# A background selection on VectorE: its steps priced anew, every fourth low part on GpSimd, the gates' sums two steps later

## The chip, the cores and the metric

The kernel runs on one core of one Trainium2 chip. The metric is the device time of one execution in microseconds (us). The shown time of the kernel before is the median of three runs, 1817.89 us (1817.82 to 1819.13).

## The reference, cut to what matters

Two layers work on 256 tokens of width 1024. Layer 0 mixes with latent attention, layer 1 with a sparse attention; each is followed by a product-key expert mixer, `_peer`, and it is inside `_peer` that the change lies:

```python
q = (xt @ w_q).reshape(T, PEER_HEADS, 2, PEER_QDIM // 2)
s1 = jnp.einsum('thd,hnd->thn', q[:, :, 0], sub_keys[0])
s2 = jnp.einsum('thd,hnd->thn', q[:, :, 1], sub_keys[1])
v1, i1 = lax.top_k(s1, PEER_TOPK)
v2, i2 = lax.top_k(s2, PEER_TOPK)
cand = (v1[..., :, None] + v2[..., None, :]).reshape(T, PEER_HEADS, -1)
cand_idx = (i1[..., :, None] * PEER_NKEYS + i2[..., None, :]).reshape(T, PEER_HEADS, -1)
best, pos = lax.top_k(cand, PEER_TOPK)
expert = jnp.take_along_axis(cand_idx, pos, axis=-1)
gate = jax.nn.softmax(best, axis=-1)
...
a = jnp.einsum('td,ted->te', x_blk, w_down[e_blk])
hg = jax.nn.gelu(a, approximate=False) * g_blk
y = jnp.einsum('te,ted->td', hg, w_up[e_blk])
```

There are 8 heads, 128 keys a half, 16 chosen of each, and 128 x 128 = 16384 experts.

## The kernel before, in words

**Dense experts.** The kernel does not gather. It multiplies all 16384 rows of `w_down` with the tokens (128 blocks of 128 rows, the tile `d`, two blocks to a PSUM tile, loop over `b0`), applies Gelu, multiplies by a matrix of gates that is zero where an expert isn't chosen (tile `G`, built by one-hot matmuls), and multiplies by `w_up` (tile `y`).

**Split operands.** Every weight block of 512 KB is loaded by SyncE into one of four `raw` buffers. ScalarE rounds it to the high part (`hi`, L105), VectorE takes the difference (`lo`, L109), and TensorE multiplies three pairs: 24 matmuls of 256 columns make one block of `pq` (the queries) or `d`, in the order hi, hi, lo. The class `Stream` keeps the parts in a ring of four slots: `get()` for block i queues the parts of block i+3 and the loads up to i+6. A slot is written again when the block four places earlier has been multiplied, and a `raw` buffer is loaded again when both its parts are made. `Stream.share` says that every so many low parts GpSimd makes one (L107) instead of VectorE; before the change it is set only in layer 1's attention (3).

**The selection in the background.** While TensorE does `pq` and the first half of `d`, VectorE chooses the experts between its low parts. `choose()` (from L1054) is a generator of steps. First come 32 rounds of `top16` over 128 scores (five instructions: MAX8, FIND_INDEX8, MATCH_REPLACE8, MAX8, FIND_INDEX8, L983 to L987). Then for each of the two tiles of 128 tokens: `pairs` (16 sums of candidates on VectorE, L1009, and 16 of indices on GpSimd, L1012, then 8 rounds of `top16` over 50 candidates), `weigh` (softmax: a subtraction L994, the exponential on ScalarE L995, then sum, reciprocal and product, L997 to L999), and `experts` (for each head a comparison on VectorE, L1026, a product on GpSimd, L1029, a reduction on VectorE, L1033). At the end `gates()` turns the two results with TensorE (tile `gT`, L1042) and makes `place16` and `gate16`.

**What sets the order.** `spend(PACE)` is called once for each block from the second pair of queries on: it adds an income to a purse and runs steps while the purse is positive, each `yield` taking its price off. All of VectorE's work here is chained in the order in which it is emitted (`dve` and `link`, L243 to L257), so the prices decide how many steps stand between two low parts. Once `spend` reports that the selection is over, `prepare` (L1094 to L1104) builds one-hot tiles for four tokens a group, and `place` multiplies them into `G`; at most two groups an iteration of two blocks, 64 in all.

Of the kernel before, what the change touches and what calls it, by code (L numbers as in the profile page):

```python
# [39 lines left out]
OFF = [sum(SEG[:a]) for a in range(TOPK)]  # L40
CELLS = sum(SEG)
STAGGER = 4
PACE = 5.75
FIRST = 4
WARM = 9
EARLY = 11264
# [123 lines left out]
def tile_trunk(ctx: ExitStack, tc: tile.TileContext, ins, out: bass.AP):  # L170
# [19 lines left out]
    def ps(name):  # L190
        return psp.tile([P, 512], F32, tag="ps", name=name)

    def py(i, name):
        return pyp.tile([P, 512], F32, tag=f"py{i}", name=name)
# [26 lines left out]
    ws = Stream(nc, raws, *ring)  # L221
# [34 lines left out]
    def dve(emit):  # L256
        return link("dve", emit)  # L257
# [4 lines left out]
    def mm(o, l, r, start, stop):  # L262
        return pe(lambda: nc.tensor.matmul(o, l, r, start=start, stop=stop, skip_group_check=True))  # L263
# [10 lines left out]
    def proj(o, blk, w=P, late=False):  # L274

        h, l = blk
        if late:
            for c in range(NC):
                mm(o, h[:, c * w : (c + 1) * w], xh[:, c, :], c == 0, False)
                mm(o, h[:, c * w : (c + 1) * w], xl[:, c, :], False, False)  # L280
            for c in range(NC):
                ins = mm(o, l[:, c * w : (c + 1) * w], xh[:, c, :], False, c == NC - 1)
            return ins
        for c in range(NC):
            s = slice(c * w, (c + 1) * w)
            ins = mm3(o, (h[:, s], l[:, s]), (xh[:, c, :], xl[:, c, :]), c == 0, c == NC - 1)
        return ins
# [639 lines left out]
    def peer(li):  # L927
# [25 lines left out]
        def turn():  # L953
            for t in range(2):
                p = ps(f"qwT{t}")
                for n in range(4):
                    nc.tensor.transpose(p[:, n * P : (n + 1) * P], qrow[t][:, n * P : (n + 1) * P], ident)
                nc.scalar.copy(qT[:, 0:4, t * P : (t + 1) * P], p.rearrange("p (n t) -> p n t", t=P))

        def queries(n):  # L960
            p = ps(f"pq{n}")
            pv = p.rearrange("p (j t) -> p j t", t=T)
            first = proj(pv[:, 0, :], ws.get())
            if n == FIRST:
                with tc.issue_after(first.ins):
                    turn()
            else:
                spend(PACE)
            proj(pv[:, 1, :], ws.get())
            if n > FIRST:  # L970
                spend(PACE)
            nc.scalar.copy(qT[:, n : n + 2, :], pv)

        def scores(g4):
            for t in range(2):
                p = py((2 * g4 + t) % 4, f"ps{g4}{t}")
                for j in range(4):
                    n = 4 * g4 + j
                    mm(p[:, j * P : (j + 1) * P], qT[:, n, t * P : (t + 1) * P], keys[:, n, :], True, True)
                nc.scalar.copy(s[t][:, 4 * g4 : 4 * g4 + 4, :], p.rearrange("p (j k) -> p j k", k=P))  # L980

        def top16(vals, ids, src, buf):
            dve(lambda: nc.vector.max(vals[:, 0:8], src))  # L983
            dve(lambda: nc.vector.max_index(ids[:, 0:8], vals[:, 0:8], src))
            dve(lambda: nc.vector.match_replace(buf, vals[:, 0:8], src, GONE))
            dve(lambda: nc.vector.max(vals[:, 8:16], buf))
            dve(lambda: nc.vector.max_index(ids[:, 8:16], vals[:, 8:16], buf))  # L987

        def weigh(t):
            bt = best[t]  # L990
            m = small.tile([P, HEADS], F32, tag="gm", name="gm")
            sm = small.tile([P, 2, HEADS], F32, tag="gs", name="gs")
            dve(lambda: nc.vector.tensor_copy(m, bt[:, :, 0]))
            dve(lambda: nc.vector.tensor_tensor(bt, bt, m[:, :, None].to_broadcast([P, HEADS, TOPK]), op=ALU.subtract))  # L994
            nc.scalar.activation(bt, bt, AF.Exp)  # L995
            yield 2
            dve(lambda: nc.vector.tensor_reduce(sm[:, 0, :], bt, axis=AX.X, op=ALU.add))  # L997
            dve(lambda: nc.vector.reciprocal(sm[:, 1, :], sm[:, 0, :]))
            dve(lambda: nc.vector.tensor_tensor(bt, bt, sm[:, 1, :, None].to_broadcast([P, HEADS, TOPK]), op=ALU.mult))  # L999
            yield 3  # L1000

        def pairs(t):
            vh = v[t].rearrange("p (h two) k -> p h two k", two=2)
            dve(lambda: nc.vector.tensor_copy(idf[t], idx[t]))
            ih = idf[t].rearrange("p (h two) k -> p h two k", two=2)
            dve(lambda: nc.vector.tensor_scalar(ih[:, :, 0, :], ih[:, :, 0, :], float(NKEYS), None, op0=ALU.mult))
            for a in range(TOPK):
                w = slice(OFF[a], OFF[a] + SEG[a])
                dve(lambda: nc.vector.tensor_tensor(cand[t][:, :, w], vh[:, :, 1, 0 : SEG[a]],  # L1009
                                                    vh[:, :, 0, a : a + 1].to_broadcast([P, HEADS, SEG[a]]),  # L1010
                                                    op=ALU.add))
                nc.gpsimd.tensor_tensor(cell[t][:, :, w], ih[:, :, 1, 0 : SEG[a]],  # L1012
                                        ih[:, :, 0, a : a + 1].to_broadcast([P, HEADS, SEG[a]]), op=ALU.add)
                if a % 4 == 3:
                    yield 3
            for h in range(HEADS):
                top16(best[t][:, h, :], pos[t][:, h, :], cand[t][:, h, :], scr()[:, :CELLS])
                yield 3
            dve(lambda: nc.vector.tensor_copy(pos16[t], pos[t]))

        def experts(t):
            held = None
            for h in range(HEADS + 1):
                if h < HEADS:
                    o, same = hot(), eq[h % 2]
                    dve(lambda: nc.vector.tensor_tensor(same, iotac,  # L1026
                                                        pos16[t][:, h, None, :].to_broadcast([P, CELLS, TOPK]),
                                                        op=ALU.is_equal))
                    nc.gpsimd.tensor_tensor(o.rearrange("p k c -> p c k"), same,  # L1029
                                            cell[t][:, h, :, None].to_broadcast([P, CELLS, TOPK]), op=ALU.mult)  # L1030
                    yield 4
                if held is not None:
                    dve(lambda: nc.vector.tensor_reduce(exp_[t][:, h - 1, :], held, axis=AX.X, op=ALU.add))  # L1033
                    yield 4
                held = o

        def gates():
# [16 lines left out]
        def choose():  # L1054
            for g4 in range(4):
                for t in range(2):
                    for n in range(4 * g4, 4 * g4 + 4):
                        top16(v[t][:, n, :], idx[t][:, n, :], s[t][:, n, :], scr())
                        yield 5
            for t in range(2):  # L1060
                yield from pairs(t)
                yield from weigh(t)
                yield from experts(t)
            yield 2 * PACE
            chains.pop("dve")
            gates()

        bg = choose()
        purse = [0]

        def spend(income):

            purse[0] += income
            while purse[0] > 0:
                cost = next(bg, None)
                if cost is None:
                    return True
                purse[0] -= cost
            return False

        chains["dve"] = None
        ws.dve = dve
        queries(4)
        scores(0)
        queries(6)
        scores(1)
# [37 lines left out]
        for b0 in range(0, NKEYS, 2):  # L1124
# [3 lines left out]
            for j in range(2):  # L1128
                proj(pv[:, j, :], ws.get())
                ready = ready or spend(PACE)  # L1130
            if b0 == 0:
# [111 lines left out]

    mla()
    peer(0)
    dsa()
    peer(1)


# [71 lines left out]
```

## Time and profile before

| | us |
|---|---|
| median of three runs | 1817.89 |
| the profiled execution | 1818.38 |
| its span on the core | 1816.6 |
| TensorE busy in it | 1793.1 |
| VectorE busy | 1362.6 |
| ScalarE busy | 1053.9 |
| GpSimd busy | 356.2 |

In the profile TensorE's matmuls are called PE, its weight loads PEld, VectorE is DVE, ScalarE is ACT, GpSimd is POOL and SyncE's queue SPq. A matmul's record is longer than the distance to the next one, since they are pipelined, so what a stage costs is read from the distance of starts or from the length of a stretch and the matmuls in it. In this execution the queries and `d` of layer 0 run from 105 us to 537 us, those of layer 1 from 1032 us to 1461 us.

### The profile page before, as it was taken

The page shows a single profiled execution, that of the slowest core. Times are in us where ns is not written, and L with a number is a line of the kernel's source. Part 1 is how long each engine was busy: PE and PEld are TensorE (multiplying, and loading weights), DVE is VectorE, ACT ScalarE, POOL GpSimd, SP SyncE. Part 2 cuts the span into 40 slices and gives each one's busy share as a digit, 9 for nine tenths or more (in the row PEclk, how much of TensorE's full clock was granted, in tenths as well). Part 3 has the DMA queues.
Part 4 walks back from the last instruction along what each step waited for, and adds up shares of the span by engine and source line. Part 5 has one row for each costly group of instructions (what it writes and reads, how often), then busy time and mean ns, then how long its engine had stood idle before and what let it go on. Part 6 is the DMA issues. An engine that isn't in the chain of part 4 may idle for free.

```text
span 1816.6 us, 32387 instructions
## 1 busy us (share of the span) xinstructions
PE 1793.1 (99%) x12495; PEld 1637.3 (90%) x12495; DVE 1362.6 (75%) x2342; ACT 1053.9 (58%) x1832; POOL 356.2 (20%) x265
## 2 busy tenths in 40 slices
PE   9999999999999999999989999999999999999998
PEld 8899999999998888888879899999999988888886
DVE  6689899788985555555679789998889965555555
ACT  6655545788864444444556554457888754444443
POOL 2000144455530000000013001343555400000000
PEclk9999999999999999999999999999999999999999
DMA  7555566445457666666646545555444576666663
GB/s 242 197 186 163 165 191 202 163 163 163 164 187 223 193 196 193 193 194 193 210 133 220 185 156 183 175 185 197 163 163 163 168 237 191 193 196 192 192 195 117
DMA packets 93468, 335.47 MB, mean 185 GB/s; under 512 B 10368, under 2 KB 11392, under 8 KB 93312
## 3 DMA queue, kind: packets, MB, share of 16 engines
q1 hardware_dynamic: 93024, 332.87, 56.4%
q8 instruction: 98, 1.61, 0.4%
q14 instruction: 58, 0.48, 0.1%
q10 hardware_dynamic: 288, 0.52, 0.1%
HBM read 329.16 MB, written 4.19 MB: 184 GB/s over the span
## 4 chain that ended last, share of the span: by engine, by line
PE 92%; DVE 6%; DMA 1%; issue 1%; ACT 1%; SPq 0%; DVEq 0%; POOLq 0%; POOL 0%; ACTq 0%
PE y L263 40%; PE d L263 34%; PE pq L263 4%; PE G L263 3%; PE q L263 3%; DVE lo L109 2%; PE v L263 2%; PE qw L263 1%; PE s L263 1%; PE ps L263 1%; PE h L263 1%; PE qi L263 1%; PE o L263 1%; DMA raw<-in_down 0%; PE qn L263 0%
## 5 line engine op out<-in xcount | busy, mean ns | idle before, releaser
L109 DVE TENSOR_TENSOR lo<-raw,hi 128x1024 fp32r<-128x1024 f32 (+1 forms) x579 | 778.7, 1347 | 279.9 <-ACT hi L105 279.1
L105 ACT CAST hi<-raw 128x1024 fp32r<-128x1024 f32 (+1 forms) x583 | 611.4, 1050 | 538.6 <-PE y L263 208.8
L263 PE MATMUL d<-xh,lo 128*128 128x256 f32 x2048 | 569.9, 278 | 7.5 <-DVE lo L109 7.5
L263 PE MATMUL d<-xh,hi 128*128 128x256 f32 x2048 | 575.0, 281 | 0.0
L263 PE MATMUL d<-xl,hi 128*128 128x256 f32 x2048 | 568.9, 278 | 0.0
L263 PEld LDWEIGHTS d<-xh,lo 128*128 128x128 f32 x2048 | 386.8, 189 | 8.8 <-DVE lo L109 8.3
L263 PEld LDWEIGHTS d<-xl,hi 128*128 128x128 f32 x2048 | 386.8, 189 | 0.0
L263 PEld LDWEIGHTS d<-xh,hi 128*128 128x128 f32 x2048 | 386.3, 189 | 0.0
L263 PE MATMUL y<-lo,xh 128*128 128x512 f32 x1088 | 337.8, 389 | 0.0
L263 PE MATMUL y<-hi,xh 128*128 128x512 f32 x1088 | 337.7, 390 | 0.0
L263 PE MATMUL y<-hi,xl 128*128 128x512 f32 x1088 | 337.3, 389 | 0.0
L1100 POOL TENSOR_TENSOR gate<-hot,gate 128x512 f16<-128x512 f16 x128 | 220.7, 1743 | 217.3 <-DVE hot L1098 217.3
L263 PEld LDWEIGHTS y<-lo,xh 128*128 128x128 f32 x1088 | 204.1, 188 | 42.7 <-DVE lo L109 0.3
L263 PEld LDWEIGHTS y<-hi,xl 128*128 128x128 f32 x1088 | 204.2, 188 | 42.5
L263 PEld LDWEIGHTS y<-hi,xh 128*128 128x128 f32 x1088 | 203.8, 188 | 41.8
L1104 ACT ACTIVATE gate<-hot,rest 128x128 f16<-128x128 f16 x512 | 166.0, 413 | 0.4 <-DVE hot L1098 0.4
L1161 ACT CAST xh<-arena 128x512 fp32r<-128x512 f32 x128 | 79.7, 624 | 145.5 <-PE y L263 145.4
L357 POOL TENSOR_TENSOR st<-st,mhalf 128x1 f32<-128x1 f32 x8 | 4.4, 549 | 800.7 <-DVE st L355 800.7
L1162 DVE TENSOR_TENSOR xl<-arena,xh 128x512 fp32r<-128x512 f32 x128 | 88.2, 692 | 73.5 <-ACT xh L1161 73.5
L1098 DVE TENSOR_TENSOR hot<-iota,place 128x1024 f16<-128x1024 f16 x128 | 84.7, 702 | 32.5 <-PE G L263 32.4
L1029 POOL TENSOR_TENSOR arena<-arena 128x800 f32<-128x800 f16 x32 | 72.6, 2276 | 105.1 <-DVE arena L1026 105.1
L263 PE MATMUL G<-gate,hot 128*128 128x128 f16 x1024 | 69.9, 221 | 0.0
(220 smaller groups left out, 1747.4 us busy)
## 6 DMA issues: line engine op xcount, KB each, us to landing
raw<-in_down SPq DMA_DIRECT2D x256, 512.0 KB, 3.3
raw<-in_up SPq DMA_DIRECT2D x256, 512.0 KB, 4.2
raw<-in_peer_q SPq DMA_DIRECT2D x24, 512.0 KB, 4.4
raw<-in_dsa_qk SPq DMA_DIRECT2D x16, 512.0 KB, 3.3
raw<-in_mla_w_o SPq DMA_DIRECT2D x8, 512.0 KB, 5.2
arena<-in_peer_q SPq DMA_DIRECT2D x8, 512.0 KB, 4.3
raw<-in_dsa_v SPq DMA_DIRECT2D x8, 512.0 KB, 4.3
raw<-in_dsa_w_o SPq DMA_DIRECT2D x8, 512.0 KB, 4.1
```

What stands on the lines that cost most here:

```text
L105: self.act(lambda: nc.scalar.copy(hi, raw))
L109: self.dve(lambda: nc.vector.tensor_tensor(lo, raw, hi.bitcast(F32), op=ALU.subtract))
L263: return pe(lambda: nc.tensor.matmul(o, l, r, start=start, stop=stop, skip_group_check=True))
L357: nc.gpsimd.tensor_tensor(st[:, 5:6], st[:, 4:5], mhalf, op=ALU.pow)
L1029: nc.gpsimd.tensor_tensor(o.rearrange("p k c -> p c k"), same, cell[t][:, h, :, None].to_broadcast([P, CELLS, TOPK]), op=ALU.mult)
L1098: nc.vector.tensor_tensor(hot, iota4[:, None].to_broadcast([P, 2, P, 4]), place16[:, :, None, four].to_broadcast([P, 2, P, 4]), op=ALU.is_ ...
L1100: nc.gpsimd.tensor_tensor(gate[:, 0], hot[:, 1].rearrange("p c j -> p j c"), gate16[:, four, None].to_broadcast([P, 4, P]), op=ALU.mult)
L1104: nc.scalar.mul(gate[:, 1, j, :], hot[:, 1, :, j], rest[:, t : t + 1])
L1161: nc.scalar.copy(hh, a)
L1162: nc.vector.tensor_tensor(al, a, hh.bitcast(F32), op=ALU.subtract)
```

## The change

Four things change, all for both layers. The prices and the income get a new scale (`PACE` 1450) and new ratios. `ws.share` is 4 from the first score matmuls (behind the first two blocks of queries) to the end of `pairs` of the first tile, and again from the end of the first tile's `experts` to the end of the second tile's `pairs`; it is 0 elsewhere in the mixer. `weigh` and `experts` of a tile are interleaved: the first two comparisons with their GpSimd products are issued between the exponential and the sum. And the order that results puts the turning of the gates (`gT`) one block later.

```diff
-PACE = 5.75
+PACE = 1450
+POOLED = 4
...
             nc.scalar.activation(bt, bt, AF.Exp)
-            yield 2
+            yield 600
             dve(lambda: nc.vector.tensor_reduce(sm[:, 0, :], bt, axis=AX.X, op=ALU.add))
...
-            yield 3
+            yield 700
...
                 if a % 4 == 3:
-                    yield 3
+                    yield (950, 450, 450, 450)[a // 4]
             for h in range(HEADS):
                 top16(best[t][:, h, :], pos[t][:, h, :], cand[t][:, h, :], scr()[:, :CELLS])
-                yield 3
+                yield 1160
...
-                    yield 4
+                    yield 1000
                 if held is not None:
                     dve(lambda: nc.vector.tensor_reduce(exp_[t][:, h - 1, :], held, axis=AX.X, op=ALU.add))
-                    yield 4
+                    yield 900
...
                         top16(v[t][:, n, :], idx[t][:, n, :], s[t][:, n, :], scr())
-                        yield 5
+                        yield 1210
             for t in range(2):
                 yield from pairs(t)
-                yield from weigh(t)
-                yield from experts(t)
+                ws.share = 0
+                gate, pick = weigh(t), experts(t)
+                yield next(gate)
+                yield next(pick)
+                yield next(pick)
+                yield from gate
+                yield from pick
+                ws.share = POOLED * (1 - t)
             yield 2 * PACE
...
         queries(4)
+        ws.share = POOLED
         scores(0)
```

Line numbers of the changed kernel are one higher from L43 to L1059 and up to eight higher below. The first place is GpSimd's queue in layer 0, from the last instruction before the mixer to the products of the first tile. Before:

```order
L357 TENSOR_TENSOR st<-st,mhalf 128x1 x2
L1012 TENSOR_TENSOR arena<-arena 128x8x16
L1012 TENSOR_TENSOR arena<-arena 128x8x8
L1012 TENSOR_TENSOR arena<-arena 128x8x5
L1012 TENSOR_TENSOR arena<-arena 128x8x4
L1012 TENSOR_TENSOR arena<-arena 128x8x3
L1012 TENSOR_TENSOR arena<-arena 128x8x2 x3
L1012 TENSOR_TENSOR arena<-arena 128x8 x8
L1029 TENSOR_TENSOR arena<-arena 128x50x16 x8
```

And of the change, the same queue's rows for the low parts (`lo`), with the 16 sums of indices (L1013) between them:

```order
L108 TENSOR_TENSOR lo<-raw_1855,hi 128x1024
L108 TENSOR_TENSOR lo<-raw_1996,hi 128x1024
L1013 TENSOR_TENSOR arena<-arena 128x8x16
L1013 TENSOR_TENSOR arena<-arena 128x8x8
L1013 TENSOR_TENSOR arena<-arena 128x8x5
L1013 TENSOR_TENSOR arena<-arena 128x8x4
L1013 TENSOR_TENSOR arena<-arena 128x8x3
L1013 TENSOR_TENSOR arena<-arena 128x8x2 x3
L1013 TENSOR_TENSOR arena<-arena 128x8 x8
L108 TENSOR_TENSOR lo<-raw_2137,hi 128x1024
L108 TENSOR_TENSOR lo<-raw_2302,hi 128x1024
L1030 TENSOR_TENSOR arena<-arena 128x50x16 x8
```

Seven low parts stand ahead of the sums (five more above these rows), two behind them, and two more in the second tile's `pairs`: 11 in each layer, 22 in all.

The second place is VectorE at the softmax of the first tile in layer 0. Before, the sum (L997) stands right behind the subtraction (L994) whose result ScalarE exponentiates:

```order
L109 TENSOR_TENSOR lo<-raw_2330,hi 128x1024
L1019 CAST arena<-arena 128x128
L993 COPY gm<-arena 128x8
L994 TENSOR_TENSOR arena<-arena,gm 128x128
L997 TENSOR_REDUCE gs<-arena 128x8
L998 RECIPROCAL gs<-gs 128x8
L999 TENSOR_TENSOR arena<-arena,gs 128x128
L1026 TENSOR_TENSOR arena<-iotac,arena 128x800
L109 TENSOR_TENSOR lo<-raw_2365,hi 128x1024
```

And of the change (subtraction L995, sum L998, comparisons L1027):

```order
L1020 CAST arena<-arena 128x128
L994 COPY gm<-arena 128x8
L995 TENSOR_TENSOR arena<-arena,gm 128x128
L110 TENSOR_TENSOR lo<-raw_2370,hi 128x1024
L1027 TENSOR_TENSOR arena<-iotac,arena 128x800 x2
L110 TENSOR_TENSOR lo<-raw_2403,hi 128x1024
L998 TENSOR_REDUCE gs<-arena 128x8
L999 RECIPROCAL gs<-gs 128x8
L1000 TENSOR_TENSOR arena<-arena,gs 128x128
```

Two low parts and two comparisons now stand between the subtraction and the sum. The third place is VectorE among the rounds over 128 scores in layer 0; before:

```order
L109 TENSOR_TENSOR lo<-raw_1373,hi 128x1024
L983 MAX arena<-arena 128x8
L984 MAX_INDEX arena<-arena 128x8
L985 MATCH_REPLACE arena<-arena 128x128
L986 MAX arena<-arena 128x8
L987 MAX_INDEX arena<-arena 128x8
L109 TENSOR_TENSOR lo<-raw_1420,hi 128x1024
```

And of the change, where the low part that stood between two rounds is GpSimd's:

```order
L110 TENSOR_TENSOR lo<-raw_1373,hi 128x1024
L984 MAX arena<-arena 128x8
L985 MAX_INDEX arena<-arena 128x8
L986 MATCH_REPLACE arena<-arena 128x128
L987 MAX arena<-arena 128x8
L988 MAX_INDEX arena<-arena 128x8
L984 MAX arena<-arena 128x8
L985 MAX_INDEX arena<-arena 128x8
L986 MATCH_REPLACE arena<-arena 128x128
L987 MAX arena<-arena 128x8
L988 MAX_INDEX arena<-arena 128x8
L110 TENSOR_TENSOR lo<-raw_1458,hi 128x1024
```

Two rounds follow one another where one block's low part is missing from VectorE. On TensorE's queue nothing moves but `gT`, 24 matmuls later in each layer; the loads and ScalarE's instructions are the same in number.

## The prediction

> **What bounds the kernel.** First the page's engine rows, then the costliest groups.
>
> ```profile
> span 1816.6 us, 32387 instructions
> PE 1793.1 (99%) x12495; PEld 1637.3 (90%) x12495; DVE 1362.6 (75%) x2342; ACT 1053.9 (58%) x1832; POOL 356.2 (20%) x265
> ...
> L263 PE MATMUL d<-xh,lo 128*128 128x256 f32 x2048 | 569.9, 278 | 7.5 <-DVE lo L109 7.5
> ```
>
> TensorE is the bound, and the change takes no matmul from it. It can gain only where TensorE waits or runs below its pace. The one wait at `d` is for VectorE's low part. Windows by stage show where (us, then PE's busy time and matmuls, the other engines, granted clock):
>
> ```profile
> core 0: us, PE busy (x) PEld busy (x) DVE busy (x) ACT busy (x) POOL busy (x), PEclk, DMA share, GB/s
> 144.61:219.05 74.44, 74.44 (x659) 74.44 (x658) 69.78 (x271) 36.83 (x44) 5.36 (x16) 1.00 0.54 177
> 219.05:232.57 13.52, 10.07 (x74) 9.87 (x73) 9.97 (x16) 6.51 (x7) 5.94 (x3) 0.87 0.37 120
> 232.57:273.37 40.80, 40.80 (x362) 40.80 (x361) 39.95 (x108) 20.80 (x24) 17.40 (x22) 1.00 0.61 194
> 273.37:282.82 9.45, 8.94 (x74) 8.50 (x73) 8.97 (x14) 5.44 (x7) 4.48 (x2) 1.00 0.49 164
> 282.82:305.44 22.62, 22.62 (x195) 22.62 (x193) 22.62 (x22) 10.27 (x12) 13.80 (x6) 1.00 0.61 197
> 305.44:323.74 18.30, 18.30 (x167) 18.25 (x165) 12.91 (x19) 11.20 (x18) 3.81 (x2) 1.00 0.68 221
> 323.74:534.11 210.37, 210.37 (x2061) 209.15 (x2058) 182.17 (x223) 168.80 (x442) 106.47 (x62) 1.00 0.50 163
> ...
> 1146.52:1159.81 13.29, 10.20 (x74) 10.00 (x73) 10.02 (x16) 6.50 (x7) 6.01 (x3) 0.87 0.38 123
> 1200.61:1209.91 9.30, 8.83 (x74) 8.44 (x73) 8.82 (x14) 5.34 (x7) 4.44 (x2) 1.00 0.48 165
> 1209.91:1231.67 21.76, 21.76 (x194) 21.76 (x193) 21.76 (x22) 10.18 (x12) 13.76 (x6) 1.00 0.61 196
> 1231.67:1249.86 18.19, 18.19 (x166) 18.15 (x165) 13.77 (x19) 11.18 (x18) 3.94 (x2) 1.00 0.72 235
> 1249.86:1458.09 208.23, 208.23 (x2060) 207.09 (x2058) 182.07 (x223) 168.93 (x442) 106.52 (x62) 1.00 0.50 165
> ```
>
> I set the edges at starts of blocks (24 matmuls). 232.57 to 273.37 holds 15 blocks: 2.72 us each. Three blocks should take 8.16. They take 13.52 at 219 (5.36 too many, at a granted clock of 0.87: the wait, and slow matmuls behind it) and 9.45 at 273 (1.29 too many). Layer 1 loses 5.13 and 1.14 likewise. After the second wait layer 0 runs 8 blocks in 22.62 instead of 21.76 (a matmul each 118 ns instead of 113) and loses 0.11 in the next row; layer 1 doesn't.
>
> What ends last there is VectorE, then ScalarE's exponential, from the timeline of both:
>
> ```profile
> 219.38 0.29 DVE L994 TENSOR_TENSOR arena<-arena,gm 128x128 f32<-128x128 f32 x1
> 223.12 0.28 DVE L997 TENSOR_REDUCE gs<-arena 128x8 f32<-128x128 f32 x1 [3.45 <-ACT arena L995]
> 224.37 1.22 DVE L109 TENSOR_TENSOR lo<-raw,hi 128x1024 fp32r<-128x1024 f32 x1
> ...
> 220.41 1.05 ACT L105 CAST hi<-raw 128x1024 fp32r<-128x1024 f32 x1 [2.45 <-DMA raw<-in_down]
> 221.48 1.28 ACT L995 ACT_TABLE_LOAD   x1
> 222.78 0.31 ACT L995 ACTIVATE arena<-arena 128x128 f32<-128x128 f32 x1
> ```
>
> VectorE's low parts are so late that the next load waits for its buffer, ScalarE's high part for the load, the exponential for both, VectorE 3.45 us for the exponential, and the low part behind it ends at 225.59, when TensorE goes on.
>
> **The change part by part.** VectorE's prices, as distances of starts:
>
> ```profile
> 157.80 0.27 DVE L983 MAX8 arena<-arena 128x8 f32<-128x128 f32 x1
> 159.36 1.21 DVE L109 TENSOR_TENSOR lo<-raw,hi 128x1024 fp32r<-128x1024 f32 x1
> 160.49 0.29 DVE L983 MAX8 arena<-arena 128x8 f32<-128x128 f32 x1
> ...
> 209.82 0.21 DVE L983 MAX8 arena<-arena 128x8 f32<-128x50 f32 x1
> 211.00 1.20 DVE L109 TENSOR_TENSOR lo<-raw,hi 128x1024 fp32r<-128x1024 f32 x1
> ```
>
> A round over 128 takes 1.56, a low part 1.13, a round over 50 takes 1.18.
>
> *Prices before.* 5.75 of income at 5 a round is 1.15 rounds a block: 1.13 + 1.79 = 2.92 us of VectorE against 2.72 of TensorE, 0.20 behind a block; 32 rounds take 28 blocks, so 5.6 us. At 3 a round over 50 it is 1.92 rounds: 1.13 + 2.26 = 3.39, 0.67 behind; 8 rounds take 4.2 blocks, so 2.8. Together 8.4. The cushion is three blocks of ring less the two parts: 8.16 - 1.05 - 1.13 = 6.0. Score matmuls give a little back; the cushion is gone about where the wait stands.
>
> *Prices after, with every fourth low part gone.* 1450/1210 is 1.20 rounds: 1.87 + 0.75 x 1.13 = 2.72, even with TensorE. 1450/1160 is 1.25 rounds over 50: 1.48 + 0.85 = 2.33, 0.39 ahead. The candidates' sums, 2.5 us in this row,
>
> ```profile
> L1009 DVE TENSOR_TENSOR arena<-arena 128x8 f32<-128x8 f32 (+6 forms) x16 | 2.5, 223 | 0.0
> ```
>
> cost 2300/1450 = 1.59 blocks: 1.57 + 0.85 = 2.42, ahead too. The experts' pair costs 1900/1450 = 1.31 blocks against 8/5.75 = 1.39, with all low parts on VectorE; the stretch from 232.57 holds this work and loses nothing, so 6% more of it eats the cushion at most slowly. VectorE thus reaches the softmax with nearly 6 us in hand instead of none. Both waits and what follows them go: 5.36 + 1.29 + 0.86 + 0.11 = 7.62 in layer 0, 5.13 + 1.14 = 6.27 in layer 1, **13.9 us**. The sum's move is part of this: two low parts and two comparisons (about 2 x 1.13 + 2 x 0.5 = 3.3 us, more where GpSimd blocks them) cover the 3.45; without that cover the wait would still fit in the cushion. The exponential itself stays in ScalarE's queue with one table load before it and one behind (1.28 each), and the high parts queued behind it are 1.28 + 0.31 + 1.28 later: 2.9 us of a lead of 8.16, so no block waits for them. This holds only while the load isn't late as it was at 220.41, which again hangs on VectorE's lead.
>
> *Low parts on GpSimd.* Layer 1's attention shows the instruction, beside VectorE:
>
> ```profile
> L107 POOL TENSOR_TENSOR lo<-raw,hi 128x1024 fp32r<-128x1024 f32 x4 | 9.6, 2398 | 36.8 <-ACT hi L105 36.8
> 978.51 4.56 DVE L109 TENSOR_TENSOR lo<-raw,hi 128x1024 fp32r<-128x1024 f32 x2
> 979.59 2.40 POOL L107 TENSOR_TENSOR lo<-raw,hi 128x1024 fp32r<-128x1024 f32 x1 [3.77 <-ACT hi L105]
> 942.42 2.40 POOL L107 TENSOR_TENSOR lo<-raw,hi 128x1024 fp32r<-128x1024 f32 x1 [27.69 <-ACT hi L105]
> 942.71 0.28 DVE L870 MATCH_REPLACE8 arena<-arena 128x128 f32<-128x128 f32 x1
> 199.41 5.36 POOL L1012 TENSOR_TENSOR arena<-arena 128x128 f32<-128x128 f32 x16 [104.70 <-DVE arena L1006]
> ```
>
> 22 x 2.40 = 53 us of GpSimd lie beside TensorE: in a pooled block hi and lo take 1.05 + 2.40 = 3.45 of the lead of 8.16, 4.7 to spare. The index sums behind pooled parts come later by up to 2.40, but their first reader is the product after the softmax. Queued behind all 16 index sums (5.36) one would be 0.7 late, at four places at most: 0 to 2.8 us, and I take 0, since they are issued four at a time. The load into such a buffer starts 2.40 - 1.13 = 1.27 later, and the loads behind it in SyncE's queue with it; from the freed buffer (3.45 into a block's lead) to the high part four blocks on are 10.88 - 3.45 = 7.4 us, against this landing time:
>
> ```profile
> raw<-in_down SPq DMA_DIRECT2D x256, 512.0 KB, 3.3
> ```
>
> That is nothing either. VectorE's second low part at 978.51 took 4.56 - 1.13 = 3.43 instead of 1.21, blocked by GpSimd: 2.2 a meeting. They meet only if VectorE begins low part k-1 after GpSimd began k, which is when it is over 2.72 behind; two rounds in one block leave it 2 x 1.56 + 1.13 - 2.72 = 1.53 behind. I take no meeting. MATCH_REPLACE8 beside GpSimd keeps its 0.28. FIND_INDEX8 beside a pooled low part isn't in the trace: between nothing and 2.4 for each; I take nothing, as the nearest row.
>
> The Trainium skill ("SBUF — State Buffer", "Who interferes with whom") says that GpSimd reading SBUF and a VectorE instruction with two SBUF inputs exclude each other whole, while one with a single input is left alone. That speaks against the change wherever low parts meet, as 3.43 shows, and for no loss in the rounds, which only the 0.28 shows here; blocked rounds would be rival A's price.
>
> *Gates one block later.* Their cover is the distance to the first `G`:
>
> ```profile
> 315.86 1.91 POOL L1100 TENSOR_TENSOR gate<-hot,gate 128x512 f16<-128x512 f16 x1 [0.69 <-DVE hot L1098]
> 323.59 1.29 DVE L1098 TENSOR_TENSOR hot<-iota,place 128x1024 f16<-128x1024 f16 x2 [1.14 <-PE G L263]
> ```
>
> The second group's gate ends at 317.77, and `G`'s 16 matmuls, about 1 us, end at 323.6: near 5 us, less 2.72, so 2 remain. Nothing. Were the cover gone, a wait of the missing part, once a layer.
>
> Sum: the profiled execution's 1818.38 (span 1816.6 and 1.8 around it) less 13.9 is 1804.5; the median lies 0.5 below that execution, so **1804.0**.
>
> **Rivals.**
> *A, slower: pooled low parts block VectorE.* From 2.72 us behind on, each pooled block costs 2.2 more, and the rounds' price, even with TensorE, pays nothing back. Nine pooled parts stand ahead of the first softmax: 19.8, less the cushion 6.0, 13.8 a layer: 1804 + 28 = 1832. For it: the 3.43. Against: the 1.53, and that a meeting the other way round, GpSimd waiting for the end of VectorE's low part, costs only GpSimd. Chance 0.05.
> *B, the slow pace spreads.* From 323.74 layer 0 takes 2.14 us more than layer 1 for the same matmuls, with no wait; one iteration in three runs at 118 ns. If the new timing puts all there, 4.3 and 6.4 come on top: 1814.7; half of it is 1809. Chance 0.12.
> *C, the slow pace goes* from layer 0 too: 1804.0 - 2.1 = 1801.9. It began there after a wait. Chance 0.20.
> *D, the change does half of what it says*: low parts in GpSimd's queue, or comparisons at their higher rate, leave a wait. Half the 13.9 stays: 1811. Chance 0.08.
>
> **How the numbers follow.** The forecast has 0.55. The range runs from C less the spread of the runs (1.3), 1800.5, to the halves of B and of what D leaves, 1809.5; outside are A, the rest of B and D, some 0.17. About 0.2% (3.6 us) is what a measurement can tell from no change: faster, below 1814.3, is the forecast, C, D and most of B, 0.91; B's end is the same, 0.04; A slower, 0.05.
>
> **What would show it.** Right: no wait of `d` for `lo`; three blocks around the softmax in 8.2 us at clock 1.00; no wait of the sum for the exponential; 26 low parts of 2.4 us on GpSimd with VectorE's neighbours at 1.21. Wrong: low parts above 2 us on VectorE among the rounds (A), a new wait for GpSimd's `lo` (D), a longer stretch from the first `G` on without waits (B).

## The result, and the profile after

The changed kernel takes 1804.47 us (median of 4 runs, 1803.02 to 1805.05); the kernel before stood at 1817.97 beside it (4 runs, 1817.82 to 1819.13). The ratio is 0.9923, 95% interval 0.9906 to 0.994: faster by 13.5 us. The profiled execution took 1804.73 for its span of 1803.0, against 1818.38 for 1816.6.

First the page of after, then its whole list of TensorE's waits (in all us, times, longest):

```profile
span 1803.0 us, 32368 instructions
PE 1786.7 (99%) x12495; PEld 1632.4 (91%) x12495; DVE 1338.9 (74%) x2320; ACT 1054.0 (58%) x1832; POOL 404.4 (22%) x287
...
PE 98%; DVE 1%; issue 1%; ACT 0%; DMA 0%; SPq 0%; DVEq 0%; POOLq 0%; POOL 0%; ACTq 0%
```

```profile
PE v L264 <- ACT hi L106: 2.7, 3, 1.2
PE idle L1206 <- DVE iotac L217: 2.5, 1, 2.5
PE v L264 <- DVE lo L110: 2.1, 3, 0.8
PE qw L264 <- DVE xl L389: 0.6, 2, 0.3
PE o L264 <- ACT arena L579: 0.3, 1, 0.3
PE h L264 <- ACT xh L1210: 0.2, 1, 0.2
PE pt L267 <- ACT arena L579: 0.2, 1, 0.2
```

No wait of `d` for `lo` is left. TensorE is 6.4 us less busy although it does the same 12495 matmuls: those that ran slowly behind the waits are gone. Behind each of the two long waits of before (3.45 us and 3.09) the granted clock was 0.50 for 3.41 us, and the matmuls came 213 ns apart instead of 113: about 1.7 us of the 5.36 that layer 0 lost there, and as much in layer 1. Windows by stage of after, columns and block edges as in the prediction:

```profile
145.32:219.76 74.44, 74.44 (x659) 74.44 (x658) 67.17 (x268) 39.40 (x47) 22.36 (x25) 1.00 0.59 191
219.76:227.92 8.16, 8.16 (x74) 8.16 (x73) 8.09 (x11) 3.91 (x5) 5.05 (x3) 1.00 0.52 169
268.72:276.88 8.16, 8.16 (x74) 8.16 (x73) 7.62 (x10) 6.52 (x7) 3.43 (x2) 1.00 0.55 188
276.88:298.64 21.76, 21.76 (x194) 21.76 (x193) 21.04 (x22) 10.40 (x12) 13.73 (x6) 1.00 0.63 208
316.73:526.91 210.18, 210.18 (x2060) 208.97 (x2058) 182.13 (x223) 168.95 (x442) 106.51 (x62) 1.00 0.49 163
1139.23:1147.39 8.16, 8.16 (x74) 8.16 (x73) 8.09 (x11) 3.92 (x5) 5.04 (x3) 1.00 0.54 163
1236.20:1444.43 208.23, 208.23 (x2061) 207.09 (x2058) 182.17 (x223) 168.83 (x442) 106.13 (x62) 1.00 0.50 165
```

Three blocks take 8.16 us at full clock where they took 13.52, 9.45 and 13.29, and the eight behind them 21.76 where layer 0 took 22.62. Added up over the whole loop of `d`, layer 0 gives 7.9 us and layer 1 6.4. The last stage of layer 0 keeps its slow pace (210.18 against 208.23).

VectorE, then ScalarE, at the first softmax of after:

```profile
214.25 0.29 DVE L995 TENSOR_TENSOR arena<-arena,gm 128x128 f32<-128x128 f32 x1
215.49 1.23 DVE L110 TENSOR_TENSOR lo<-raw,hi 128x1024 fp32r<-128x1024 f32 x1 [0.95 <-ACT hi L106]
216.63 1.05 DVE L1027 TENSOR_TENSOR arena<-iotac,arena 128x800 f16<-128x800 f16 x2
218.26 1.95 DVE L110 TENSOR_TENSOR lo<-raw,hi 128x1024 fp32r<-128x1024 f32 x1 [0.57 <-ACT hi L106]
220.13 0.28 DVE L998 TENSOR_REDUCE gs<-arena 128x8 f32<-128x128 f32 x1
```

```profile
214.41 1.05 ACT L106 CAST hi<-raw 128x1024 fp32r<-128x1024 f32 x1 [1.18 <-PE d L264]
215.48 1.28 ACT L996 ACT_TABLE_LOAD   x1
216.77 0.31 ACT L996 ACTIVATE arena<-arena 128x128 f32<-128x128 f32 x1
```

The high part no longer waits for a load, VectorE waits for the high part instead of TensorE for VectorE, and the sum at 220.13 waits for nothing. The low part that ends at 216.72 is block 28's. TensorE reads it 0.23 us into that block, at 222.71 (block 28 starts 2.72 behind 219.76). This distance, from the end of a low part to its first use, here 6.0 us, is called the **lead** below. A lead below 0 means that TensorE waits. I worked it out for every block by pairing the traces' low parts and blocks in order:

| layer 0, lead in us at block | 3 | 20 | 27 | 28 | least, at block |
|---|---|---|---|---|---|
| before | 7.8 | 1.4 | 0.2 | -3.6 | -3.6, 28 |
| after | 7.8 | 4.6 | 6.0 | 6.0 | 4.1, 52 |

Layer 1 of after goes down to 2.6 at block 21, and comes back.

### The profile page after: what moved, and what is told of

Its sections match the earlier page's. It is cut to its first block, busy times and chain, and to the rows that moved or that the text cites. A ratio compares the mean times of both kernels' runs of the same rounds, so it can differ in the third digit from the quotient of the medians.

```text
span 1803.0 us, 32368 instructions
## 1 busy us (share of the span) xinstructions
PE 1786.7 (99%) x12495; PEld 1632.4 (91%) x12495; DVE 1338.9 (74%) x2320; ACT 1054.0 (58%) x1832; POOL 404.4 (22%) x287
## 4 chain that ended last, share of the span: by engine, by line
PE 98%; DVE 1%; issue 1%; ACT 0%; DMA 0%; SPq 0%; DVEq 0%; POOLq 0%; POOL 0%; ACTq 0%
PE y L264 41%; PE d L264 39%; PE pq L264 4%; PE G L264 3%; PE q L264 3%; PE v L264 2%; PE qw L264 1%; PE s L264 1%; PE ps L264 1%; PE h L264 1%; PE qi L264 1%; PE o L264 1%; PE qn L264 0%; DMA arena<-in_xT 0%; PE kn L264 0%
## 5 line engine op out<-in xcount | busy, mean ns | idle before, releaser
L110 DVE TENSOR_TENSOR lo<-raw,hi 128x1024 fp32r<-128x1024 f32 (+1 forms) x557 | 750.7, 1349 | 291.2 <-ACT hi L106 289.5
L108 POOL TENSOR_TENSOR lo<-raw,hi 128x1024 fp32r<-128x1024 f32 x26 | 62.8, 2414 | 223.8 <-ACT hi L106 223.8
```

Source lines behind the costliest of these rows:

```text
L108: nc.gpsimd.tensor_tensor(lo, raw, hi.bitcast(F32), op=ALU.subtract)
L110: self.dve(lambda: nc.vector.tensor_tensor(lo, raw, hi.bitcast(F32), op=ALU.subtract))
```

## Experiments

Theory T, from the prediction: VectorE's lead is used up by the rounds and the candidates; it takes the pooled low parts to keep it; the sums' move covers the exponential. Rival P: the prices do it. All ratios below are to runs of before on the same chip (1818.4 to 1819.5 there). "27 to 30" are three blocks, 8.16 us without a wait.

### Parts undone, parts alone

The change without pooled parts:

```diff
-POOLED = 4
+POOLED = 0
```

> The change without low parts on GpSimd (share stays 0); prices and moved sums kept. Theory T (the missing low parts carry the gain): VectorE needs 1.13 + 1.20 x 1.56 = 3.00 us a block against 2.72, 0.28 behind for 26.7 blocks of rounds = 7.5 us, over the cushion of 6.0: TensorE waits at d for lo again, before the candidates, about 1 to 2 us in each layer; time 1806 to 1810. Rival P (the prices carry it): no wait of d, 1803 to 1805.5.

1804.9 (1803.97 to 1806.36), ratio 0.9921 (0.9895 to 0.9946), and no wait of `d`: rival P's time, not T's. The lead is 1.3 at block 20, 1.8 at 27, 2.9 at 28, at least 1.0 (block 52). So pooled parts (low parts made by GpSimd) raise the lead (6.0 against 1.8 at block 27), but here nothing uses the rest.

The change with the sums right behind the exponential:

```diff
-                gate, pick = weigh(t), experts(t)
-                yield next(gate)
-                yield next(pick)
-                yield next(pick)
-                yield from gate
-                yield from pick
+                yield from weigh(t)
+                yield from experts(t)
```

> The change with the sums put back right behind the exponential. Theory T: VectorE waits for the exponential again, up to 3.5 us, but has 5 to 6 us in hand there: no wait of d, 1803 to 1806. Rival S: d waits for lo at the softmax, 1807 to 1812.

1803.81 (1803.01 to 1804.58), ratio 0.9913 (0.9888 to 0.9937). As T said, the exponential is back among VectorE's waits and is paid from the lead, with no wait of `d`. It is 0.40 at the first softmax of each layer, where a low part falls between the subtraction and the sum, and 2.57 at the second, where none does (lead 6.0 at block 47, 3.1 at 48):

```profile
DVE gs L998 <- ACT arena L996: 5.9, 4, 2.6
```

Before with pooled parts alone (`share` set and cleared where the change does, old prices, sums not moved):

```diff
+POOLED = 4
...
                 yield from pairs(t)
+                ws.share = 0
                 yield from weigh(t)
                 yield from experts(t)
+                ws.share = POOLED * (1 - t)
...
+        ws.share = POOLED
         scores(0)
```

> The kernel before with every fourth low part on GpSimd in the same stretches; old prices, sums right behind the exponential. Theory T: rounds take 1.79 + 0.85 = 2.64 of 2.72, candidates' rounds 2.26 + 0.85 = 3.11, 0.39 behind for 4.2 blocks = 1.6, within the cushion: no wait of d for lo, the sum's wait for the exponential stays on VectorE alone; 1803 to 1806. Rival P (the prices carry it): the overload of the candidates' rounds keeps a wait of 3 us a layer, 1810 or more. Rival S (the moved sums carry it): the wait of 3.45 for the exponential reaches d, 1810 or more.

1807.46 (1804.58 to 1809.27), ratio 0.9929 (0.9902 to 0.9956): 12.1 us less than before, nearly all of the gain, and between T's range and the rivals'. Layer 0 loses nothing. Layer 1 has one wait of `d`, 0.5 us, and small losses at both softmaxes (8.32 for 27 to 30, 8.89 for 45 to 48). Its lead was shortened where pooled parts met VectorE's, most of all at block 24 (3.5 at block 23, 0.9 at 24):

```profile
1129.85 3.06 DVE L110 TENSOR_TENSOR lo<-raw,hi 128x1024 fp32r<-128x1024 f32 x1
1129.42 2.41 POOL L108 TENSOR_TENSOR lo<-raw,hi 128x1024 fp32r<-128x1024 f32 x1 [4.01 <-ACT hi L106]
```

Before with the sums moved alone (the interleaving of the diff, without `share`):

> The kernel before with only the sums moved two steps on. Theory T: VectorE is still 8.4 us behind against a cushion of 6.0 at the softmax, so both waits of d stay, shorter by what the exponential added: 1 to 2 us each in place of 3.6 and 0.8; 1809 to 1815. Rival S (the wait for the exponential was the cause): no wait, 1803 to 1806.

1812.86 (1809.22 to 1814.77), ratio 0.9964 (0.9953 to 0.9975). Half the gain, as T said: VectorE no longer waits for the exponential, but its low parts are late all the same (lead -1.2 at block 29). Blocks 27 to 30, 45 to 48 and 48 to 56:

```profile
218.89:228.63 9.74, 8.68 (x74) 8.48 (x73) 9.64 (x15) 6.40 (x7) 4.21 (x3) 1.00 0.49 161
...
269.75:278.67 8.92, 8.46 (x75) 8.26 (x73) 8.82 (x13) 5.18 (x7) 5.18 (x2) 1.00 0.52 175
278.67:301.04 22.37, 22.04 (x194) 21.84 (x193) 22.37 (x22) 10.40 (x12) 13.78 (x6) 1.00 0.57 190
```

### The prices, and one of them

The change with both undone, `POOLED` 0 and `weigh` ahead of `experts`, so that only the prices are left:

> The kernel after, but with no low part given to GpSimd and with the gates' sums right behind the exponential again: of the change only the prices are left. Theory Q (the lead decides, and VectorE's wait for the exponential is paid from it): without pooled parts VectorE's lead over TensorE was 1.8 us at block 27; a wait of 2.6 to 3.5 us for the exponential is more than that, so TensorE waits 0.8 to 1.7 us at the softmax in each layer, and 0 to 0.5 at the second: 1806 to 1808.5. Rival R (the prices alone are enough, as the high parts and not VectorE set the low parts there): no wait of d, 1803.5 to 1805.5.

1804.24 (1803.18 to 1805.8), ratio 0.9924 (0.9902 to 0.9947): all of the gain, which is rival R's range. Q was wrong about the exponential. The lead is as without pooled parts (1.3 at block 20, 1.8 at 27, 2.9 at 28; at least 0.7), yet the exponential costs VectorE 0.5 us and not 2.6 to 3.5. VectorE and ScalarE at the first softmax of this kernel:

```profile
217.61 0.29 DVE L995 TENSOR_TENSOR arena<-arena,gm 128x128 f32<-128x128 f32 x1
217.82 1.22 DVE L110 TENSOR_TENSOR lo<-raw,hi 128x1024 fp32r<-128x1024 f32 x1
219.52 0.29 DVE L998 TENSOR_REDUCE gs<-arena 128x8 f32<-128x128 f32 x1 [0.48 <-ACT arena L996]
```

```profile
216.32 1.05 ACT L106 CAST hi<-raw 128x1024 fp32r<-128x1024 f32 x1 [1.67 <-PE d L264]
217.27 0.59 ACT L1139 ACTIVATE arena<-d 128x512 f32<-128x512 f32 x1
217.88 1.28 ACT L996 ACT_TABLE_LOAD   x1
219.17 0.31 ACT L996 ACTIVATE arena<-arena 128x128 f32<-128x128 f32 x1
```

The high part ahead of the exponential waits for TensorE only (before: 2.45 us for a load, at 220.41), so ScalarE is free for the table load when VectorE's subtraction ends; and with these prices a low part happens to fall between subtraction and sum. The table load needs nothing of VectorE: at the second softmax of this kernel it starts at 269.07, 2.4 us ahead of the subtraction (271.46), and VectorE's wait is 0.38 with nothing in between. What the exponential costs thus hangs on how far ScalarE's queue has come when VectorE gets there. Here that is luck of the prices; nothing in them aims at it.

That kernel with one price put back, a candidates' round at 757 of 1450, which is 3 of 5.75:

```diff
-                yield 1160
+                yield 757
```

> Prices alone, as in the kernel that stood at 1804.2, with one of them put back: a candidates' round costs 757 of 1450 again, 1.92 rounds a block. Theory Q (this one price makes the lead vanish, and the wait for the exponential grows out of the vanished lead, since the high part ahead of the exponential then waits for a late load): lead 1.3 us at block 20, 0.67 less a block for 4 blocks, so below 0 at block 27; VectorE waits 2.5 to 3.5 us for the exponential; blocks 27 to 30 take 11.5 to 14 us, 45 to 48 9 to 9.5: 1812 to 1818. Rival V (the new prices of the sums, the gates and the experts do as much): blocks 27 to 30 below 9.5, below 1808.

1820.9 (1818.01 to 1824.21), ratio 1.0013 (1.0001 to 1.0025): the whole gain is gone with this one number, and the time lies above Q's range. The form was not as expected either. The waits don't stand at 27 to 30 (8.95) but begin among the candidates, in the window of blocks 0 to 27, and are many and small; layer 0, and then TensorE's wait for `lo`:

```profile
144.52:222.26 77.74, 75.42 (x659) 74.82 (x658) 72.47 (x278) 39.76 (x47) 7.31 (x17) 1.00 0.51 169
222.26:231.21 8.95, 8.45 (x74) 8.25 (x73) 8.95 (x9) 3.65 (x4) 6.55 (x4) 1.00 0.54 179
...
273.98:283.69 9.71, 8.45 (x74) 8.25 (x73) 9.71 (x10) 3.64 (x4) 6.11 (x4) 1.00 0.48 159
```

```profile
PE d L264 <- DVE lo L110: 9.1, 12, 1.5
```

The lead goes 1.3 at block 20, 0.2 at 23, -0.6 at 24, -1.6 at 26.

The same price put back in the full change (pooled parts and moved sums stay):

> The kernel after with that same price alone put back (757 instead of 1160): pooled parts and moved sums stay. Theory Q: the pooled parts give VectorE a lead of 4 us or more ahead of the candidates, which take 2 to 3 us of it, and the sums wait for nothing: no wait of d above 0.3 us, 1803.5 to 1806. Rival V: the price is needed whatever else is changed: blocks 27 to 30 above 9.5, above 1807.

1809.15 (1808.95 to 1812.45), ratio 0.9952 (0.9936 to 0.9968): V's range, but not V's place. Q holds at the first softmax (8.16 in both layers) and fails at the second, ahead of which two more low parts are pooled, against eight or nine ahead of the first: blocks 45 to 48 take 8.94 and 9.06, and layer 1's blocks 30 to 45 take 43.71. `d` waits for `lo` four times, 3.2 us in all. Pooled parts meet VectorE's there; GpSimd, VectorE and ScalarE:

```profile
1170.68 2.39 POOL L108 TENSOR_TENSOR lo<-raw,hi 128x1024 fp32r<-128x1024 f32 x1 [1.10 <-ACT hi L106]
1171.71 2.44 DVE L110 TENSOR_TENSOR lo<-raw,hi 128x1024 fp32r<-128x1024 f32 x1
1177.46 1.05 ACT L106 CAST hi<-raw 128x1024 fp32r<-128x1024 f32 x1 [4.18 <-DMA raw<-in_down]
```

The low part of 1171.71 is 1.2 longer than one alone, TensorE stands for it (its next matmul starts 1.95 us behind the last one), and behind it ScalarE's high part stands 4.18 us for a load. With a short lead a pooled part can cost what it saves: 1.2 us here, against the 1.13 of a low part taken from VectorE.

Before with one number changed, a candidates' round of the first table at 4.6 of 5.75 (1.25 rounds a block); the second table's stay at 3:

```diff
-                yield 3
+                yield 4.6 if t == 0 else 3
```

> The kernel before with one number changed: a candidates' round of the first table costs 4.6 of the 5.75 a block instead of 3, so 1.25 rounds a block instead of 1.92. Sums not moved, no pooled parts, the second table's rounds as before. Theory Q: the lead no longer shrinks from 1.4 us at block 20 to nothing, but stays at 1.3 to 2; the exponential then takes 1.3 to 2.2 us of TensorE's time at the first softmax (blocks 27 to 30 in 9.5 to 10.5 instead of 13.5) and the second table keeps its 1.2 or so: 1809 to 1812.5. Rival R (the candidates' price was the whole matter): blocks 27 to 30 in 8.2, the second table's wait alone left, 1806 to 1807.5.

1812.18 (1810.58 to 1814.66), ratio 0.9962 (0.995 to 0.9974). Q's time, with the loss in other places than Q said: blocks 0 to 30 are clean in both layers (lead 2.5 at 27, 2.9 at 28); VectorE then waits 2.59 us for the exponential, which is paid behind block 30, and the second table spends what is left (lead -1.3 at block 48). The 2.59 is what the exponential costs with the load in time, no low part in between, and a high part and the table load still to come in ScalarE's queue, as the high part and the sum show:

```profile
221.65 1.05 ACT L105 CAST hi<-raw 128x1024 fp32r<-128x1024 f32 x1 [1.67 <-PE d L263]
224.35 0.29 DVE L997 TENSOR_REDUCE gs<-arena 128x8 f32<-128x128 f32 x1 [2.59 <-ACT arena L995]
```

Before had 3.45 there, so the late load was worth some 0.9 of it. Blocks 27 to 30, 30 to 45 and 48 to 56 of layer 0:

```profile
218.84:227.00 8.16, 8.16 (x74) 8.16 (x73) 5.37 (x19) 6.35 (x7) 0.00 (x0) 1.00 0.45 151
227.00:268.27 41.27, 41.17 (x363) 40.97 (x361) 40.79 (x83) 19.75 (x24) 22.59 (x24) 1.00 0.57 192
...
276.43:300.46 24.03, 22.32 (x194) 21.93 (x193) 24.00 (x25) 12.12 (x14) 15.87 (x7) 1.00 0.57 189
```

That kernel with the sums moved as well:

> The one above with the gates' sums moved behind the first two comparisons too: two small edits, no pooled parts. Theory Q: the exponential is covered, blocks 27 to 30 take 8.2 to 8.4; the second table still draws at 1.92 rounds a block and keeps 0.7 to 1.3 us in blocks 45 to 56 of each layer: 1806 to 1808. Rival S (the lead kept at the first softmax also carries the second table): no wait of d longer than 0.3 us, 1803.5 to 1805.5.

1806.56 (1806.29 to 1807.9), ratio 0.9935 (0.9913 to 0.9957): Q's range. The waits have nearly gone (lead at least 0.2 in layer 0, -0.2 in layer 1, both at block 50). The loop of `d` is still 0.9 and 2.2 us longer than after's. In layer 1 the 2.2 is nearly all a slower pace of the matmuls, which that layer doesn't have in after: one pair of blocks in three takes 6.63 us instead of 6.45, some eleven times, 2.0 in all.

Every second low part pooled:

```diff
-POOLED = 4
+POOLED = 2
```

> The kernel after with every second low part on GpSimd instead of every fourth. Theory Q: VectorE's lead is not short in the kernel after, so more of it buys nothing: no wait of d, 1803.5 to 1805.5. Rival A (pooled parts that meet VectorE's, or stand behind the index sums, make low parts late): low parts of 2 to 3.4 us on VectorE in each block, waits of d for lo, above 1807.

1804.16 (1803.08 to 1805.92), ratio 0.9924 (0.9901 to 0.9947), no wait of `d`, as Q said. GpSimd makes 43 low parts in the mixers (47 with the four of the attention), and TensorE's time doesn't move. The lead falls to 1.0 at one place, where VectorE's low part took 3.1.

```profile
L108 POOL TENSOR_TENSOR lo<-raw,hi 128x1024 fp32r<-128x1024 f32 x47 | 113.7, 2419 | 194.1 <-ACT hi L106 194.1
```

## Why the prediction was right, and where its steps were not

**Time and place: right.** 13.9 us were to come from the two softmaxes of each layer, 7.62 in layer 0 and 6.27 in layer 1; the loop gave 7.9 and 6.4. That is 14.3; but the first block of `d` starts 0.7 later in after's profile (145.32 against 144.61), behind the same code, hence 13.65 between the profiled executions.

**That VectorE's lead decides: right.** The kernels whose lead stays well above 0 in both layers stand at 1803.8 to 1804.9, whichever edit did it, and the "nearly 6 us in hand" at the softmax is what the trace of after has (6.0). The others lose where their lead is gone; three of them also have the slower pace in layer 1.

**What keeps the lead: wrong.** The step that failed is "Prices after, with every fourth low part gone", with the 8.4 against a cushion of 6.0 ahead of it. The prediction added the prices up only with the pooled parts in them, and by its own numbers the rounds without them fall 0.28 behind a block (1.20 x 1.56 + 1.13 = 3.00 against 2.72). The runs without the pooled parts, without the move and without both give the same time. The forecast came true all the same because both waits vanish whole, whichever edit keeps the lead; in that its number was lucky. Of its terms:
- The cushion of 6.0 is right: the lead stands at 6.0 at block 5 of layer 0, before and after, and after comes back to it. The fall from 7.8 at block 3 is the same in both, so it isn't the rounds'.
- The rounds took 4.6 of the 6.0 by block 20, not 5.6. The rounds' new price takes as much (6.0 to 1.3 without pooled parts), so this edit saves nothing.
- The candidates' 1.92 rounds a block took 1.8 (2.0 at block 23, 0.2 at 27), not 2.8. Ahead of the exponential the lead was thus just used up, and not 8.4 - 6.0 = 2.4 overdrawn: TensorE's wait of 3.45 (3.09 in layer 1) is almost wholly VectorE's wait for the exponential (3.45 and 3.17), with nothing left to pay it.
- At 1.25 rounds a block without pooled parts VectorE gets ahead (1.3 at 20, 1.8 at 27, 2.9 at 28): 1.48 + 1.13 = 2.61 against 2.72, where the prediction had worked out only the 2.33 with them. Among the prices this is the one that carries the gain. With the other prices new, the kernel stands 14.2 us below before with it and 2.2 above before without it, each measured on its own chip. Whether it is enough with every other price old wasn't tried; raised in the first table alone it is worth 6.2.
- Had the sum been made for the prices alone, from the lead of block 20 on, it would have shown a lead above 0 as far as the exponential. That this then costs 0.5 and not the 3.45 is in no term of it. The pooled parts do nearly the same with the old prices (12.1 us), so the two edits stand in for each other.

**The sums' move: right as a cover, not needed.** It takes the wait of 3.45 away, and alone is worth half. With the other edits there, the wait is 2.6 at most, and 0.4 to 0.5 where a low part falls in between or the table is loaded already; the lead pays for either.

**Low parts on GpSimd: priced right.** They take 2.41 us on average, and the lead at most pooled blocks of after is 4.7, as 8.16 less 3.45 said; no round beside them got longer. One met VectorE in layer 1, behind the index sums:

```profile
1113.81 4.39 POOL L1013 TENSOR_TENSOR arena<-arena 128x128 f32<-128x128 f32 x16 [6.26 <-DVE arena L1007]
1118.15 2.39 POOL L108 TENSOR_TENSOR lo<-raw,hi 128x1024 fp32r<-128x1024 f32 x1
1118.37 0.20 DVE L988 FIND_INDEX8 arena<-arena 128x8 uint32<-128x50 f32 x1
1118.64 2.98 DVE L110 TENSOR_TENSOR lo<-raw,hi 128x1024 fp32r<-128x1024 f32 x1
```

The search at 1118.37 keeps its 0.20 beside GpSimd, so the bound taken as nothing was nothing; the low part with two inputs stands until GpSimd ends at 1120.54. "I take no meeting" was thus wrong: VectorE was not 2.72 behind, but GpSimd was late, behind all 16 index sums, which the prediction had set aside as 0.7 us at most. The lead paid for it (2.6 at block 21). The rule of the Trainium skill ("SBUF — State Buffer", "Who interferes with whom") that the prediction weighed is that a VectorE instruction with two SBUF inputs and a GpSimd one that reads SBUF lock each other out, while one with a single input doesn't contend unless it runs in a two-port mode. It agrees with these rows, 2.98 and 0.20. The prediction left the two-port modes out; the last section has a row for them.

**Gates: right.** The second gate ends at 313.58 and the first `G` starts at 315.84, 2.3 us of cover against the 2 of the prediction.

**Rivals.** A (pooled parts block VectorE) did not come in the full change, but its mechanism is real where the lead is short, in the two pooled runs with the old candidates' price: low parts of 3.06 and 2.44 us, and TensorE waiting right behind the second and seven blocks behind the first. D did not come. B did not come in after; the slow pace did reach layer 1 in three experiments. C fell: layer 0 keeps its slow pace in all runs, also in the five that have no wait of `d` at all, so its premise ("it began there after a wait") was wrong.

## What to carry to other kernels

Where one engine feeds another through a ring of buffers, follow the lead, the time from the end of each piece to its use, over the whole stage: the wait shows where the lead ends, the cause is where it was spent, here largely by a price that let in 1.92 rounds a block instead of 1.25. A change that comes as a bundle wants each part priced alone, with the others absent; here the prices did all of the work alone, the pooled parts alone nearly all, the move half, and together they were worth no more than the prices. And a wait's length depends on what stands around it: the exponential cost VectorE 3.45 us behind a late load, 2.6 behind one in time, and 0.4 to 0.5 where a low part stood in between or ScalarE had loaded its table already, so it has to be read anew for the order that the change will have.

## What was not expected of the hardware

A long wait cost more than its length. Behind the waits of 3.45 and 3.09 us in before the granted clock was 0.50 for 3.41 us, while in the experiments, where no wait of `d` was longer than 1.7, it is 1.00 in every window of the queries' and `d`'s stages shown here. What sets this wasn't tried.

The matmuls have two paces that no wait explains. In layer 0's last stage one pair of blocks in three runs at 118 ns a matmul from end to end, the other two change to 113 ns within some seven matmuls of their start; a pair takes 6.63 instead of 6.45 us. Layer 1 runs the same instructions without such a pair, except in three runs, the two with the candidates' price raised in the first table alone and the one with prices alone and the candidates' put back, where both layers show the pattern. It costs some 2 us a layer. What sets it wasn't tried and stays open.

A cast with a single input stood for GpSimd too, in the full change with the old candidates' price, at 1163.37: 128x256 in 1.59 us, against 0.29 for the same one in its other three places, while a pooled part ran from 1161.46 to 1164.81. The sum of a row (L1034) just before it kept its 0.97 beside the same part.

```profile
1162.47 0.97 DVE L1034 TENSOR_REDUCE arena<-arena 128x16 f32<-128x800 f32 x1
1163.37 1.59 DVE L1005 CAST arena<-arena 128x256 f32<-128x256 uint32 x1
1161.46 3.35 POOL L108 TENSOR_TENSOR lo<-raw,hi 128x1024 fp32r<-128x1024 f32 x1
```

The same section of the Trainium skill ("SBUF — State Buffer", "Who interferes with whom") says that casts can enter a two-port mode, in which they take the port pair that VectorE shares with GpSimd, and that a row's sum (`tensor_reduce`) never does on this chip. Both rows agree: 1.59 against 0.29, and 0.97 kept.

Kernels with waits also scatter more from run to run: 1815.4 to 1823.7 for before and 1818.0 to 1824.2 with the old candidates' price, 1803.0 to 1806.4 for those without a wait.
